# Mixture of softmaxes: two engines copy both column halves to the same partitions, whole-row-pair stores, and six output groups held for the end

## The chip, the cores and the metric

The kernel runs on one core of a Trainium2 chip. The time is device microseconds of one execution. Three runs of the kernel before gave 792.81, 792.83 and 791.32 us, a median of 792.81.

A core has five engines that run side by side and wait for each other by semaphores: TensorE (PE; its weight loads are shown as PEld) multiplies matrices and writes to PSUM, VectorE (DVE), ScalarE (ACT) and GpSimd (POOL) work on tiles, and SyncE (SP) issues transfers. Transfers between DRAM and SBUF are carried by 16 DMA engines. SBUF and PSUM have 128 partitions.

## The reference

For each of 32 x 128 = 4096 rows there are four heads of 4096 logits and four prior weights. A softmax is taken over each head, the prior is turned into a softmax over the heads, and the output row is the weighted sum of the four softmaxes:

```python
prior_probs = np.exp(prior - prior.max(axis=-1, keepdims=True))
prior_probs = prior_probs / prior_probs.sum(axis=-1, keepdims=True)
softmax = np.exp(logits - logits.max(axis=-1, keepdims=True))
softmax = softmax / softmax.sum(axis=-1, keepdims=True)
mixture = np.sum(prior_probs[..., None] * softmax, axis=2)
```

All of it is float32. The logits are 268 MB, the output is 67 MB.

## The kernel before

**Tiles and groups.** The 4096 output rows are cut into 32 groups (g) of 128 rows. A group is two tiles (j = 0, 1) of 64 rows: row m of tile j is row 2m + j of the group, so the two tiles of a group interleave by rows. There are N = 64 tiles; tile n belongs to group n // 2. A tile's load (`load`, L66 to L72, issued by SP at L70) brings 64 rows x 4 heads into 128 partitions: partition 2m + q holds heads 2q and 2q + 1 of row m, 32 KB, 4 MB in all. Five SBUF slots hold tiles. The last six tiles use only slots 4, 0, 1 and 2 (`slot`, L63), so that slot 3 is free from tile 53 on.

**One tile's work.** For each of the two heads i in a partition, `top` (L74) takes the max over 4096 columns on VectorE (L76) and then the exponentials in place on ScalarE, with their sum (L79). `weigh` (L83) takes the reciprocal of the sum on VectorE (L84), makes a 128 x 64 weight matrix on GpSimd from a 0/1 matrix, the reciprocal and the prior's weight (L86), and issues 16 matmuls (L93), 8 pairs of 64 x 512. These add the two partitions of a row and, over i = 0 and 1, the two heads. The column halves of 2048 go to different PSUM partitions: columns 0 to 2047 of the 64 rows stand in partitions 0 to 63 of the accumulator, columns 2048 to 4095 in partitions 64 to 127. There are two accumulators of four PSUM banks, taken in turn.

**Eviction and stores.** `evict` (L112) copies an accumulator to SBUF with one ScalarE instruction of 128 x 2048 (L113). The SBUF buffer `obuf` has 128 partitions x 2 groups' halves; a group's output keeps the column halves on their own partitions. So a store (`store`, L115, through `part`, L100) takes two DMAs of 1 MB, one per column half, each of 64 partitions with two pieces of 8 KB per partition (one for each j). ScalarE issues both.

**The order.** It is written out by hand. The loop of tile n does: `top(n, 0)`; the second half of the tile before, `weigh(w, 1)` with w = n - 1; the load that takes tile w's slot; `top(n, 1)`; `weigh(n, 0)`; then `evict(w)`, and, if w closes a group below `HOLD`, the group's store. Each engine runs its instructions in this order.

**The end.** With `HOLD = G - 4 = 28`, groups 28 and 29 are not stored when they are done: they are kept in slot 3, and their stores are issued after the last load, one column half by SP (in the loop with w = N - 3) and the other by ScalarE (at n = N - 2). Groups 30 and 31 go to `obuf` and are stored in pieces by both queues, the last tile in two halves of 1024 columns.

Of the kernel before, what the change touches and what calls it, by code (L numbers as in the profile page):

```python
# [13 lines left out]
M = 64  # L14
J = 2
Q = 2
BANK = 512
SLOTS = 5


@with_exitstack
def kernel(
    ctx: ExitStack,
    tc: tile.TileContext,
    logits: bass.AP,
    prior: bass.AP,
    out: bass.AP,
):
    nc = tc.nc
    B, S, H, V = logits.shape  # L30
    R = M * J
    G = B * S // R
    N = G * J
    W = V // 2
    assert G * R == B * S and G == 32 and H == 2 * Q and V == 8 * BANK


    lg = logits.rearrange("b s h v -> (b s) h v").rearrange(
        "(g m j) (q i) v -> g j m q (i v)", m=M, j=J, i=Q
    )  # L40
    ov = out.rearrange("b s v -> (b s) v").rearrange("(g m j) v -> g m j v", m=M, j=J)
    pv = prior.rearrange("b s h -> (b s) h").rearrange("(g r) h -> g r h", r=R)

    cpool = ctx.enter_context(tc.tile_pool(name="cpool", bufs=1))
    psum = ctx.enter_context(tc.tile_pool(name="psum", bufs=1, space=bass.MemoryType.PSUM))

    slots = [cpool.tile([P, Q, V], FP32, name=f"slot{i}") for i in range(SLOTS)]

    obuf = cpool.tile([P, J, V], FP32, name="obuf")
    accs = [psum.tile([P, W], FP32, name=f"acc{i}") for i in range(2)]  # L50

    sel = cpool.tile([P, M], FP32, name="sel")
    wts = [[cpool.tile([P, M], FP32, name=f"wt{k}{i}") for i in range(Q)] for k in range(2)]
    pr = cpool.tile([G, R, H], FP32, name="pr")
    pn = cpool.tile([G, J, Q, M, Q], FP32, name="pn")
    pmax = cpool.tile([G, R], FP32, name="pmax")
    pp = cpool.tile([P, J, Q, G], FP32, name="pp")
    nmax = [cpool.tile([P, N], FP32, name=f"nmax{i}") for i in range(Q)]
    dsum = [cpool.tile([P, N], FP32, name=f"dsum{i}") for i in range(Q)]
    rden = [cpool.tile([P, N], FP32, name=f"rden{i}") for i in range(Q)]  # L60


    def slot(n):  # L63
        return slots[n % SLOTS if n < N - 6 else (4, 0, 1, 2)[(n - N + 6) % 4]]

    def load(n):  # L66
        src = lg[n // J, n % J]
        for i in range(0, Q, Q if n < N - 1 else 1):
            k = Q if n < N - 1 else 1
            nc.sync.dma_start(  # L70
                out=slot(n)[:, i : i + k], in_=src[:, :, i * V : (i + k) * V]
            )  # L72

    def top(n, i):  # L74
        x = slot(n)[:, i]
        nc.vector.tensor_reduce(  # L76
            out=nmax[i][:, n : n + 1], in_=x, axis=AX.X, op=ALU.max, negate=True
        )
        nc.scalar.activation(  # L79
            x, x, AF.Exp, bias=nmax[i][:, n : n + 1], accum_out=dsum[i][:, n : n + 1]  # L80
        )

    def weigh(n, i):  # L83
        nc.vector.reciprocal(rden[i][:, n : n + 1], dsum[i][:, n : n + 1])  # L84
        wt = wts[n % 2][i]
        nc.gpsimd.tensor_scalar(  # L86
            out=wt, in0=sel, scalar1=rden[i][:, n : n + 1],
            scalar2=pp[:, n % J, i, n // J : n // J + 1], op0=ALU.mult, op1=ALU.mult,
        )

        for b in range(W // BANK):
            for c in range(2):
                nc.tensor.matmul(  # L93
                    accs[n % 2][c * M : (c + 1) * M, b * BANK : (b + 1) * BANK],
                    lhsT=wt,
                    rhs=slot(n)[:, i, c * W + b * BANK : c * W + (b + 1) * BANK],
                    start=i == 0, stop=i == Q - 1,
                )

    def part(eng, g, c, js=slice(0, J), lo=0, hi=W):  # L100
        eng.dma_start(  # L101
            out=ov[g, :, js, c * W + lo : c * W + hi],
            in_=home(g)[c * M : (c + 1) * M, js, lo:hi],
        )

    HOLD = G - 4

    def home(g):
        x = slots[3] if HOLD <= g < G - 2 else obuf
        return x[:, g % 2].rearrange("p (j w) -> p j w", j=J)  # L110

    def evict(n, lo=0, hi=W):  # L112
        nc.scalar.copy(home(n // J)[:, n % J, lo:hi], accs[n % 2][:, lo:hi])  # L113

    def store(g):  # L115
        for c in range(2):
            part(nc.scalar, g, c)

    def prior_user(n):
        return max(k for k in range(n) if slot(k) is slot(n))  # L120

    with tc.manual_schedule():
        for n in range(SLOTS):
            load(n)
        nc.scalar.dma_start(out=pr, in_=pv)

        nc.gpsimd.memset(sel, 1.0)  # L127
        nc.gpsimd.affine_select(  # L128
            out=sel, in_=sel, compare_op=ALU.is_ge, fill=0.0, base=0,
            pattern=[[-Q, M]], channel_multiplier=1,  # L130
        )
        nc.gpsimd.affine_select(  # L132
            out=sel, in_=sel, compare_op=ALU.is_ge, fill=0.0, base=Q - 1,
            pattern=[[Q, M]], channel_multiplier=-1,
        )

        nc.vector.reduce_max(pmax, pr, axis=AX.X)  # L137
        nc.vector.tensor_sub(pr, pr, pmax.unsqueeze(2).to_broadcast([G, R, H]))  # L138
        nc.scalar.activation(pr, pr, AF.Exp)  # L139
        nc.vector.reduce_sum(pmax, pr, axis=AX.X)  # L140
        nc.vector.reciprocal(pmax, pmax)  # L141
        prv = pr.rearrange("g (m j) (q i) -> g j i m q", j=J, i=Q)
        pmv = pmax.rearrange("g (m j) -> g j m", j=J)
        for j in range(J):
            for i in range(Q):
                nc.vector.tensor_mul(  # L146
                    pn[:, j, i], prv[:, j, i], pmv[:, j].unsqueeze(2).to_broadcast([G, M, Q])
                )
        pq = pn.rearrange("g j i m q -> g j i (m q)")
        for t in range(P // 32):  # L150
            nc.vector.transpose(  # L151
                pp[32 * t : 32 * (t + 1)], pq[:, :, :, 32 * t : 32 * (t + 1)]
            )

        for n in range(N):
            w = n - 1
            top(n, 0)
            if n == N - 2:
                for g in (HOLD, HOLD + 1):
                    part(nc.scalar, g, 1)  # L160
            if w >= 0:
                weigh(w, 1)
                for k in range(SLOTS, N):
                    if prior_user(k) == w:
                        load(k)
                if w == N - 3:
                    for g in (HOLD, HOLD + 1):
                        part(nc.sync, g, 0)
            top(n, 1)
            weigh(n, 0)  # L170
            if w >= 0:
                evict(w)
                g = w // J
                if w % J == J - 1 and g < HOLD:
                    store(g)
                elif w == N - 3 or w == N - 2:
                    js = slice(0, J) if w == N - 3 else slice(0, 1)
                    part(nc.sync, g, 0, js)
                    part(nc.scalar, g, 1, js)

        n = N - 1
        weigh(n, 1)
        for lo in (0, W // 2):
            evict(n, lo, lo + W // 2)
            part(nc.sync, n // J, 0, slice(1, 2), lo, lo + W // 2)
            part(nc.scalar, n // J, 1, slice(1, 2), lo, lo + W // 2)
# [30 lines left out]
```

## Time and profile before

| What | Value |
|---|---|
| Median of three runs | 792.81 us |
| Profiled execution | 793.28 us, span 791.6 us, granted TensorE clock 0.873 |
| Busy, share of the span | PE 69%, DVE 72%, ACT 76%, POOL 7% |
| Bytes | 335.95 MB in all, mean 424 GB/s |
| SP's queue | 272.63 MB, 80.4% of 16 engines' span |
| ACT's queue | 62.98 MB, 19.1% of 16 engines' span |
| VectorE's idle time ahead of the max (L76) | 194.6 us, ended by the loads |
| ScalarE's idle time ahead of the exponentials (L79) | 178.0 us, ended mostly by the max |
| Load of a tile, issue to landing | 38.0 us, median |
| Store of 1 MB by ACT, issue to landing | 21.5 us, median |

The span is the time on the profile's clock between the first and the last event of the program. Engines' busy times overlap, so shares do not add up to one. The line of the DMA engines' use in 40 slices tells whether transfers fill the span; the timeline of one engine tells, in brackets behind an instruction, how long the engine stood idle before it and what ended that.

### The profile page before, as it was taken

The page shows a single profiled execution, that of the slowest core. Times are in us where ns is not written, and L with a number is a line of the kernel's source. Part 1 is how long each engine was busy: PE and PEld are TensorE (multiplying, and loading weights), DVE is VectorE, ACT ScalarE, POOL GpSimd, SP SyncE. Part 2 cuts the span into 40 slices and gives each one's busy share as a digit, 9 for nine tenths or more (in the row PEclk, how much of TensorE's full clock was granted, in tenths as well). Part 3 has the DMA queues.
Part 4 walks back from the last instruction along what each step waited for, and adds up shares of the span by engine and source line. Part 5 has one row for each costly group of instructions (what it writes and reads, how often), then busy time and mean ns, then how long its engine had stood idle before and what let it go on. Part 6 is the DMA issues. An engine that isn't in the chain of part 4 may idle for free.

```text
span 791.6 us, 5426 instructions
## 1 busy us (share of the span) xinstructions
PE 548.0 (69%) x2048; PEld 160.4 (20%) x2048; DVE 573.3 (72%) x268; ACT 600.2 (76%) x323; POOL 51.6 (7%) x135
## 2 busy tenths in 40 slices
PE   0777568776687765767766767677578776687884
PEld 0222112221122221222211222222122221122221
DVE  5986867767768668677686676776867867768890
ACT  1897777787787787877877778778777787787894
POOL 0000000000000000000000000000000000000000
PEclk9999997899978899888999798789997799977897
DMA  9999999999999999999999999999999999999997
GB/s 376 442 416 431 431 428 430 432 431 427 434 432 435 429 432 436 430 433 431 434 429 433 431 431 429 428 435 431 429 431 432 431 432 433 433 430 436 429 416 229
DMA packets 18841, 335.95 MB, mean 424 GB/s; under 512 B 2144, under 2 KB 2144, under 8 KB 2432
## 3 DMA queue, kind: packets, MB, share of 16 engines
q1 hardware_dynamic: 10032, 272.63, 80.4%
q10 hardware_dynamic: 8784, 62.98, 19.1%
q8 instruction: 16, 0.26, 0.1%
q14 instruction: 9, 0.07, 0.0%
HBM read 268.50 MB, written 67.11 MB: 424 GB/s over the span
## 4 chain that ended last, share of the span: by engine, by line
DMA 73%; PE 12%; DVE 10%; ACT 2%; issue 1%; POOL 1%; ACTq 0%; SPq 0%; POOLq 0%
DMA slot<-in_logits_dram 73%; PE acc L93 12%; DVE nmax L76 10%; ACT slot L79 1%; POOL wt L86 1%; ACT obuf L113 1%; ACTq L101 0%; DVE rden L84 0%; SPq L70 0%; POOLq L86 0%; ACTq L79 0%; ACTq L113 0%
## 5 line engine op out<-in xcount | busy, mean ns | idle before, releaser
L93 PE MATMUL acc<-slot,wt 128*64 128x512 f32 x2048 | 548.0, 693 | 235.3 <-POOL wt L86 235.3
L76 DVE TENSOR_REDUCE nmax<-slot 128x1 f32<-128x4096 f32 x128 | 563.5, 4410 | 194.6 <-DMA slot<-in_logits_dram 194.6
L79 ACT ACTIVATE slot<-slot,nmax 128x4096 f32<-128x4096 f32 x128 | 474.6, 3708 | 178.0 <-DVE nmax L76 175.4
L93 PEld LDWEIGHTS acc<-slot,wt 128*64 128x64 f32 x2048 | 160.4, 158 | 622.0 <-POOL wt L86 311.8
L113 ACT COPY obuf<-acc 128x2048 f32<-128x2048 f32 (+1 forms) x61 | 110.9, 1817 | 4.8 <-PE acc L93 4.2
L86 POOL TENSOR_SCALAR wt<-sel,rden,pp 128x64 f32<-128x64 f32 x128 | 50.8, 397 | 725.7 <-DVE rden L84 721.8
L84 DVE RECIPROCAL rden<-dsum 128x1 f32<-128x1 f32 x128 | 19.6, 153 | 6.0 <-ACT slot L79 6.0
L79 ACT ACTIVATION_READ_ACCUMULATOR slot<-slot,nmax 128x1 f32 x128 | 23.9, 186 | 0.0
L113 ACT COPY slot<-acc 128x2048 f32<-128x2048 f32 x4 | 7.4, 1844 | 0.0
L137 DVE TENSOR_REDUCE pmax<-pr 32x128 f32<-32x512 f32 x1 | 0.7, 674 | 2.7 <-DMA pr<-in_prior_dram 2.7
L139 ACT ACT_TABLE_LOAD x1 | 1.3, 1283 | 1.2 <-PEq L201 1.2
L139 ACT ACTIVATE pr<-pr 32x512 f32<-32x512 f32 x1 | 0.6, 628 | 1.6 <-DVE pr L138 1.6
L151 DVE STREAM_TRANSPOSE pp<-pn 32x128 f32<-32x128 f32 x4 | 1.2, 302 | 0.1
L140 DVE TENSOR_REDUCE pmax<-pr 32x128 f32<-32x512 f32 x1 | 0.7, 674 | 0.7 <-ACT pr L139 0.7
L141 DVE RECIPROCAL pmax<-pmax 32x128 f32<-32x128 f32 x1 | 0.9, 942 | 0.0
L146 DVE TENSOR_TENSOR pn<-pr,pmax 32x128 f32<-32x128 f32 x4 | 0.9, 274 | 0.0
L138 DVE TENSOR_TENSOR pr<-pr,pmax 32x512 f32<-32x512 f32 x1 | 0.7, 678 | 0.0
L128 POOL TENSOR_SCALAR_AFFINE_SELECT sel<-sel 128x64 f32<-128x64 f32 x1 | 0.2, 241 | 0.1
L132 POOL TENSOR_SCALAR_AFFINE_SELECT sel<-sel 128x64 f32<-128x64 f32 x1 | 0.2, 240 | 0.1
L127 POOL MEMSET sel<- 128x64 f32 x1 | 0.2, 153 | 0.3 <-POOLq L201 0.3
L201 POOL MEMSET const-float32-0.0<- 128x1 f32 x1 | 0.1, 99 | 0.3 <-issue 0.3
L201 POOL MEMSET const-bfloat16-1.0<- 128x1 bf16 x1 | 0.1, 102 | 0.0
(2 smaller groups left out, 0.2 us busy)
## 6 DMA issues: line engine op xcount, KB each, us to landing
slot<-in_logits_dram SPq DMA_DIRECT2D x63, 4096.0 KB, 38.0
out_dram<-obuf ACTq DMA_DIRECT2D x57, 1024.0 KB, 21.5
slot<-in_logits_dram SPq DMA_DIRECT2D x2, 2048.0 KB, 20.2
out_dram<-slot SPq DMA_DIRECT2D x2, 1024.0 KB, 24.3
out_dram<-slot ACTq DMA_DIRECT2D x2, 1024.0 KB, 12.2
out_dram<-obuf SPq DMA_DIRECT2D x1, 1024.0 KB, 11.2
out_dram<-obuf SPq DMA_DIRECT2D x1, 512.0 KB, 4.3
out_dram<-obuf ACTq DMA_DIRECT2D x1, 512.0 KB, 6.2
```

Source lines behind the costliest of these rows:

```text
L76: nc.vector.tensor_reduce(out=nmax[i][:, n : n + 1], in_=x, axis=AX.X, op=ALU.max, negate=True)
L79: nc.scalar.activation(x, x, AF.Exp, bias=nmax[i][:, n : n + 1], accum_out=dsum[i][:, n : n + 1])
L84: nc.vector.reciprocal(rden[i][:, n : n + 1], dsum[i][:, n : n + 1])
L86: nc.gpsimd.tensor_scalar(out=wt, in0=sel, scalar1=rden[i][:, n : n + 1], scalar2=pp[:, n % J, i, n // J : n // J + 1], op0=ALU.mult, op1= ...
L93: nc.tensor.matmul(accs[n % 2][c * M : (c + 1) * M, b * BANK : (b + 1) * BANK], lhsT=wt, rhs=slot(n)[:, i, c * W + b * BANK : c * W + (b + ...
L113: nc.scalar.copy(home(n // J)[:, n % J, lo:hi], accs[n % 2][:, lo:hi])
L137: nc.vector.reduce_max(pmax, pr, axis=AX.X)
L138: nc.vector.tensor_sub(pr, pr, pmax.unsqueeze(2).to_broadcast([G, R, H]))
L139: nc.scalar.activation(pr, pr, AF.Exp)
L141: nc.vector.reciprocal(pmax, pmax)
L146: nc.vector.tensor_mul(pn[:, j, i], prv[:, j, i], pmv[:, j].unsqueeze(2).to_broadcast([G, M, Q]))
L151: nc.vector.transpose(pp[32 * t : 32 * (t + 1)], pq[:, :, :, 32 * t : 32 * (t + 1)])
```

## The change

Groups 0 to 29 are evicted otherwise. The output buffer gives a group 64 partitions, the even groups the lower and the odd groups the upper ones, and all 2 x 4096 columns of a row pair stand side by side on one partition. So both column halves of an accumulator are copied to the same 64 partitions. The copy is cut at column 1536 (`CUT`, three of the four banks): ScalarE copies 64 x 1536 twice, once per half, and VectorE copies 64 x 512 twice. `declare_no_dep` keeps the two engines from waiting for each other, and dependencies added by hand make each copy wait for the store two groups before, and each store wait for all copies of its group.

A row pair of the output, rows 2m and 2m + 1, is contiguous in DRAM, 32 KB. A group's store is now one DMA of 64 x 32 KB, issued by ScalarE. `HOLD` goes from 28 to 26: groups 26 and 27 stay in `obuf`, 28 and 29 in slot 3, and two DMAs of 4 MB on SP (`store_two`) store them after the last load. Groups 30 and 31 are evicted and stored as before, but into the slot of tile 60 (slot 1), since `obuf` is held.

```diff
+CUT = 3 * BANK
...
-    HOLD = G - 4
+
+    HOLD = G - 6
+    SPLIT = G - 2
+    copies = {}
+    stores = {}
 
     def home(g):
-        x = slots[3] if HOLD <= g < G - 2 else obuf
+        x = obuf if g < G - 4 else slots[3] if g < SPLIT else slot(SPLIT * J)
+        if g < SPLIT:
+            return x[(g % 2) * M : (g % 2 + 1) * M]
         return x[:, g % 2].rearrange("p (j w) -> p j w", j=J)
 
+    def after(ins, other):
+        tc.add_manual_dep(
+            ins.ins, other.ins.name,
+            mybir.DependencyInfo(mybir.DependencyClass.Sync, mybir.DependencyReason.DATA),
+            reason="kept by hand",
+        )
+
+    def apart(ins, g):
+        done = copies.setdefault(g, [])
+        for other in done:
+            if other.ins.engine != ins.ins.engine:
+                tc.declare_no_dep(
+                    ins.ins, other.ins, reason="other columns of the output tile"
+                )
+        if g - 2 in stores:
+            after(ins, stores[g - 2])
+        done.append(ins)
+
     def evict(n, lo=0, hi=W):
-        nc.scalar.copy(home(n // J)[:, n % J, lo:hi], accs[n % 2][:, lo:hi])
+        acc = accs[n % 2]
+        g = n // J
+        dst = home(g)[:, n % J]
+        if g >= SPLIT:
+            nc.scalar.copy(dst[:, lo:hi], acc[:, lo:hi])
+            return
+        for c in range(2):
+            apart(nc.scalar.copy(dst[:, c * W : c * W + CUT], acc[c * M : (c + 1) * M, :CUT]), g)
+        for c in range(2):
+            apart(
+                nc.vector.tensor_copy(
+                    dst[:, c * W + CUT : (c + 1) * W], acc[c * M : (c + 1) * M, CUT:]
+                ),
+                g,
+            )
 
     def store(g):
-        for c in range(2):
-            part(nc.scalar, g, c)
+        stores[g] = nc.scalar.dma_start(out=ov[g], in_=home(g))
+        for ins in copies[g]:
+            after(stores[g], ins)
+
+
+    def store_two(g):
+        x = obuf if g < G - 4 else slots[3]
+        ins = nc.sync.dma_start(
+            out=ov[g : g + 2].rearrange("g m j v -> (g m) j v"), in_=x
+        )
+        for k in (g, g + 1):
+            for other in copies[k]:
+                after(ins, other)
...
             top(n, 0)
-            if n == N - 2:
-                for g in (HOLD, HOLD + 1):
-                    part(nc.scalar, g, 1)
...
                 if w == N - 3:
-                    for g in (HOLD, HOLD + 1):
-                        part(nc.sync, g, 0)
+                    store_two(HOLD)
+                    store_two(HOLD + 2)
```

## The prediction

> **What bounds the kernel now.** I write S(n) for the moment at which VectorE starts the first max of tile n (L76). First the page's slices: are the DMA engines ever idle?
>
> ```profile
> DMA  9999999999999999999999999999999999999997
> GB/s 376 442 416 431 431 428 430 432 431 427 434 432 435 429 432 436 430 433 431 434 429 433 431 431 429 428 435 431 429 431 432 431 432 433 433 430 436 429 416 229
> ```
>
> They are full but for the last slice: transfers bound the body, and the last slice carries 229 GB/s. The stages by window (columns: length, busy time and count of PE, PEld, DVE, ACT, POOL, then clock, DMA share, GB/s):
>
> ```profile
> 23.29:42.71 19.42, 16.54 (x66) 4.79 (x66) 17.75 (x8) 16.80 (x10) 1.59 (x4) 1.00 1.00 432
> 602.00:626.22 24.22, 18.79 (x68) 5.46 (x66) 17.75 (x9) 18.69 (x11) 1.59 (x4) 0.79 1.00 430
> 735.27:754.70 19.43, 15.75 (x66) 4.65 (x64) 17.75 (x9) 16.47 (x11) 1.58 (x4) 0.91 0.99 428
> 776.00:791.60 15.60, 7.23 (x28) 2.02 (x24) 0.16 (x1) 5.07 (x5) 0.40 (x1) 0.72 0.68 194
> ```
>
> A pair of tiles with its output group (602 row) takes 24.22 us, 12.1 us a tile; where no stores run (23 and 735 rows) a tile takes 9.71 us. In the last 15.6 us the DMA share is 0.68: here the last tile's arithmetic is awaited. So the end is a race between transfers and the compute chain. That chain by VectorE's timeline:
>
> ```profile
> 735.27 4.42 DVE L76 TENSOR_REDUCE nmax<-slot 128x1 f32<-128x4096 f32 x1 [2.90 <-DMA slot<-in_logits_dram]
> 739.61 0.15 DVE L84 RECIPROCAL rden<-dsum 128x1 f32<-128x1 f32 x1
> 739.68 4.40 DVE L76 TENSOR_REDUCE nmax<-slot 128x1 f32<-128x4096 f32 x1
> 743.99 0.15 DVE L84 RECIPROCAL rden<-dsum 128x1 f32<-128x1 f32 x1
> 745.00 4.42 DVE L76 TENSOR_REDUCE nmax<-slot 128x1 f32<-128x4096 f32 x1 [0.85 <-DMA slot<-in_logits_dram]
> 754.70 4.42 DVE L76 TENSOR_REDUCE nmax<-slot 128x1 f32<-128x4096 f32 x1 [0.83 <-DMA slot<-in_logits_dram]
> ```
>
> VectorE needs 8.8 us of a tile and then waits for the load. TensorE's timeline (one line per unbroken burst; 32 are the last half of tile n-1 and the first of tile n):
>
> ```profile
> 619.25 9.85 PE L93 MATMUL acc<-slot,wt 128*64 128x512 f32 x32 [3.33 <-POOL wt L86]
> 643.47 3.65 PE L93 MATMUL acc<-slot,wt 128*64 128x512 f32 x16 [3.33 <-POOL wt L86]
> 740.40 8.78 PE L93 MATMUL acc<-slot,wt 128*64 128x512 f32 x32 [2.00 <-POOL wt L86]
> 759.84 3.65 PE L93 MATMUL acc<-slot,wt 128*64 128x512 f32 x16 [1.67 <-POOL wt L86]
> ```
>
> Sixteen matmuls take 3.65 us at full clock (F); in a merged burst the first sixteen take 8.78 - 3.65 = 5.13 (M) or about 9.85 - 3.65 = 6.2 (S, clock low from the start). From 520 to 630 us nine successive tiles are two F, five M, two S. ScalarE's PSUM copies by shape:
>
> ```profile
> L113 ACT COPY obuf<-acc 128x2048 f32<-128x2048 f32 x59 | 108.8, 1845 | 0.0
> L113 ACT COPY obuf<-acc 128x1024 f32<-128x1024 f32 x2 | 2.0, 1012 | 4.8 <-PE acc L93 4.2 <-ACT obuf L113 0.6
> ```
>
> **The change part by part.** *The split eviction on ScalarE.* 60 copies of 2048 columns become 120 of 1536: by the two rows 1012 + 512 x 0.813 ns = 1.43 us each, 2.86 a tile for 1.85, +1.0 us x 60. ScalarE's tile is then 2 x 3.71 + 2.86 = 10.3 us (plus 0.6 us of DMA issue in every second), under the 12.1 us of the body: hidden there by its idle time before L79 (178 us), and in the last stage by VectorE's chain below. Were that cover gone, it would pace the last stage at 10.3 us.
>
> *The new work on VectorE.* 120 copies of 512 columns. No row shows VectorE reading PSUM. The page's nearest in engine and columns:
>
> ```profile
> L138 DVE TENSOR_TENSOR pr<-pr,pmax 32x512 f32<-32x512 f32 x1 | 0.7, 678 | 0.0
> ```
>
> I take 2 x 0.678 = 1.35 us a tile. Ends: below, 512 columns at the max's rate (4.34/4096) without fixed cost, 2 x 0.54 = 1.1; above, each with another 0.18 us, the fixed part of ScalarE's PSUM copy (2 x 1.012 - 1.845), 2 x 0.86 = 1.72.
>
> *The new wait.* These copies wait for the last sixteen matmuls of tile n-1, and behind them on VectorE stands the max of tile n+1, for which ScalarE's exp waits. The matmuls start 740.40 - 735.27 = 5.13 us after S(n) and end at 8.78 (F), 10.26 (M) or 11.3 (S); the reciprocal ahead of the copies ends at 743.99 + 0.15 - 735.27 = 8.87. So VectorE needs per tile C = 10.2 (F: 8.87 + 1.35), 11.6 (M) or 12.7 (S). In the body the mix gives (2 x 10.2 + 5 x 11.6 + 2 x 12.7)/9 = 11.5 us against 12.1: the loads still set the pace, with 0.6 us to spare, and a late tile costs nothing since loads land 38 us after issue, three tiles ahead. ScalarE's new wait for VectorE's copies before a store is over before its own end (S(n) + 15.5).
>
> *The stores.* One 2 MB issue in place of two of 1 MB: ScalarE's queue loses one issue of 0.6 us per group, which its idle time hid. 32 KB against 32 KB packets of loads should give a store half the engines where 8 KB against 32 KB gave it a fifth: a store is through in about 10 us, not 24. The bytes per second: a pair with stores moves 10.49 MB in 24.22 us = 433 GB/s, loads alone 4.194/9.71 = 432, so 8 KB packets cost nothing now and I take 0. Ends: the ACT queue's bytes at the SP queue's price (19.1% for 62.98 MB against 80.4% for 272.63) would save 2.8% of 151 us, of it 26/32 groups, -3.4 us; the lowest slice of the body (427 for 431) laid to the stores alone, a fifth of the bytes, +1.4.
>
> *Two more groups held.* Before the last loads 2 x 2.097 MB less is moved: 4.194/0.431 = 9.7 us. Tile 62 would land at 745.0 for 754.7, and tiles 55 on every 9.7 us, as long as their slots are free: load 63 goes out after the last matmul of tile 59, S(60) + 10.3 = 742.5 at the C taken below, still before 745.0. But VectorE now paces these tiles. S(54): 662.57 now; the store of group 25, issued at 652.75 and at a fifth, was 40% through then; at half it is through, 0.6 x 2.097/0.431 = 2.9 us more ahead of tile 54: S(54) = 665. Copies run in loops 54 to 60, seven of them: S(61) = 665 + 7C against 745.0. After tile 61 VectorE has no more copies and ScalarE is the chain as before, with the loads already there: the 0.39 us before the exp at 763.54 and some 0.1 go, -0.5. End moved by 7C - 80.5.
>
> Which C? After idle times of TensorE of up to 1.67 us every burst was F, after 1.95 to 2.26 us M, S only after 3.3 or more. The idle time here is C less the burst, 2.2 (F) to 2.9 us (M): no S, and mostly M. I take the body's ratio, five M to two F: C = 11.2, S(61) = 743.4, **-2.1 us**. All M: C = 11.6, +0.7. All F: 10.2, -9.1, cut by the drain.
>
> [...] The burst at 740.40, after 2.00 us, ran slow at first, so I go by the row.
>
> *The drain.* Loads end at 745.0 + 9.7 = 754.7; the six groups, 12.58 MB/0.431 = 29.2 us, end at 783.9, and at least 3.0 us (shortest landing of a store) follow: 786.9 for 791.6, so no gain over 4.7 us. The first 4 MB store stands on SP right behind the last load, the second waits for tile 59's copies (S(59) + 15.5 = 736.5), early enough; behind them are only the last groups' halves. The last pieces, issued about then, share the engines with little.
>
> **Sum.** The profiled run took 793.28 (span 791.6 and 1.7 around it), 0.5 above the median 792.81. 793.28 - 2.1 - 0.5 = 790.7.
>
> **Rivals.** [...] *A wash*: C between 11.3 and 11.7, all or nearly all M; -1.6 to +1.6, 791.2 to 794.4; for it the M after every idle time of two us. *VectorE becomes the bound* (other side): the pair of copies costs p. From p = 1.47 with all M (10.26 + p), or 1.87 with five M, C is 11.73 and the end later by 0.2%: +1.6 us, 794.4. At the upper end p = 1.72, all M: C = 12.0, +3.4 us, 796.2. From p = 1.95 (C = 12.1 in the body) the body itself falls behind: each 0.1 us costs 5.8 us more, and a longer tile lengthens TensorE's idle time towards S, 1.1 us a tile; p = 2.05, all M, gives 7 x 12.3 - 80.5 + 5.8 = +11.4, 804.2. For it: no row shows this copy, and the margin is 0.6 us; against it: the 512-column rows. *Better packets*: -3.4 more, 787.3; against it the equal rates.
>
> **How the numbers follow.** Forecast as told (a gain of 1.6 to 4.7 us with C from 10.8 to 11.27): 0.34; drain or better packets: 0.12; wash: 0.18; VectorE the bound: 0.36. So faster by over 0.2% 0.46, within (1.6 us, about what a measurement of this kernel tells from no change) 0.18, slower 0.36. The forecast's own range is 788.1 to 791.2. With both signs held, the range goes from 787.3 (better packets) to 799, between the last two prices of the VectorE case; beyond lie some 0.2.
>
> **What would show it.** VectorE copies near 0.68 us x120 and ScalarE's near 1.43 x120; tiles still 12.1 us apart in the body, with loads ending VectorE's waits; from tile 54 on VectorE idle for TensorE and not for loads, S(61) near 743; a DMA share near 1 until about 784. Wrong if a VectorE copy takes 0.8 us or more, if S is common after 660 us, or if the body's pair takes other than 24.2 us.

## The result, and the profile after

The changed kernel takes 829.22 us (four runs, 828.75 to 834.09), the kernel before 792.07 us (791.11 to 792.83 beside them): a ratio of 1.048, 95% interval 1.044 to 1.053. It is 37 us slower, where 2 us less was forecast. The profiled run took 834.09 us (span 832.4), 41 us over that of before. A run more than 1.5% above the fastest of its kernel is left out of medians and ratios; of the runs told here this concerns one of e5.

First the slices of the page, as before: are the DMA engines idle, and what do they move?

```profile
DMA  9999999999999999999999999999999999698997
GB/s 381 430 424 416 413 431 419 412 417 409 430 398 418 414 403 414 412 409 406 411 402 421 406 415 418 406 413 409 397 418 427 415 419 392 287 392 355 412 402 269
```

They are as full as before in the body, but the row of rates has changed from 430 or so in every slice to values between 397 and 431. A late VectorE would leave gaps; busy engines that move less point elsewhere. Now two windows of the changed kernel with the columns of the prediction (length, busy time and count of PE, PEld, DVE, ACT, POOL, then clock, DMA share, GB/s). The first lies ahead of the first store, which is issued at 50.1 us; the second reaches from the start of tile 8 to that of tile 52:

```profile
23.29:42.71 19.42, 16.45 (x56) 4.79 (x58) 18.33 (x9) 17.03 (x10) 1.19 (x3) 0.91 1.00 432
107.93:681.11 573.18, 381.95 (x1418) 111.31 (x1414) 450.88 (x265) 463.65 (x268) 34.90 (x88) 0.85 1.00 413
```

And the same 44 tiles in the kernel before:

```profile
102.90:638.33 535.43, 381.53 (x1410) 111.69 (x1408) 390.55 (x176) 411.55 (x221) 34.89 (x88) 0.86 1.01 432
```

Loads alone still run at 432 GB/s. As soon as stores run, the rate is 413 for 432, at a DMA share of 1.00 (1.01 before): 573.2 us for 535.4, 38 us more, or 0.86 us a tile. Tile 8 itself starts 5 us later (107.93 for 102.90). From tile 52 to the end the changed kernel needs 151.3 us against 153.3. The three parts, 5.0 + 37.8 - 2.0, are the 40.8 us between the spans. (The other three runs of the changed kernel took 828.75 to 829.58 us; so some 5 us of the 41 are this run's own.) The loss lies in the stretches where stores of 2 MB run beside loads, and the rest, from tile 52 on, got 2 us shorter.

The groups of the page say what VectorE waited for (columns: busy time, mean ns of one, then idle time ahead of them and what ended it):

```profile
L77 DVE TENSOR_REDUCE nmax<-slot 128x1 f32<-128x4096 f32 x128 | 563.3, 4408 | 64.0 <-DMA slot<-in_logits_dram 63.3
L145 ACT COPY obuf<-acc 64x1536 f32<-64x1536 f32 x112 | 160.5, 1433 | 2.0
L148 DVE COPY obuf<-acc 64x512 f32<-64x512 f32 x112 | 77.2, 689 | 83.7 <-PE acc L94 81.3
```

Both copies have the predicted price: 1433 ns for 1.43 us, 689 ns for 0.678. VectorE now waits 81.3 us for TensorE ahead of its copies, the wait of which the prediction spoke, and still 63.3 us for loads ahead of the max. An engine that waits for loads is not the bound, though it lost most of its 194.6 us of such waits.

### The profile page after: what moved, and what is told of

It is laid out like the page before. It is cut to its first block, busy times and chain, and to the rows that moved or that the text cites. A ratio compares the mean times of both kernels' runs of the same rounds, so it can differ in the third digit from the quotient of the medians.

```text
span 832.4 us, 5668 instructions
## 1 busy us (share of the span) xinstructions
PE 548.6 (66%) x2048; PEld 160.0 (19%) x2048; DVE 655.4 (79%) x388; ACT 666.8 (80%) x383; POOL 51.6 (6%) x135
## 4 chain that ended last, share of the span: by engine, by line
DMA 61%; DVE 16%; PE 15%; ACT 4%; issue 2%; POOL 1%; ACTq 0%; POOLq 0%; SPq 0%
DMA slot<-in_logits_dram 61%; PE acc L94 15%; DVE nmax L77 14%; ACT slot L80 3%; DVE obuf L148 1%; POOL wt L87 1%; ACT obuf L145 1%; ACT slot L142 1%; DVE slot L148 1%; ACT slot L145 0%; DVE rden L85 0%; ACTq L102 0%; POOLq L87 0%; SPq L71 0%; ACTq L80 0%
## 5 line engine op out<-in xcount | busy, mean ns | idle before, releaser
L77 DVE TENSOR_REDUCE nmax<-slot 128x1 f32<-128x4096 f32 x128 | 563.3, 4408 | 64.0 <-DMA slot<-in_logits_dram 63.3
L145 ACT COPY obuf<-acc 64x1536 f32<-64x1536 f32 x112 | 160.5, 1433 | 2.0
L148 DVE COPY obuf<-acc 64x512 f32<-64x512 f32 x112 | 77.2, 689 | 83.7 <-PE acc L94 81.3
L145 ACT COPY slot<-acc 64x1536 f32<-64x1536 f32 x8 | 11.5, 1434 | 0.1
L142 ACT COPY slot<-acc 128x2048 f32<-128x2048 f32 (+1 forms) x5 | 7.6, 1517 | 4.8 <-PE acc L94 4.2
L148 DVE COPY slot<-acc 64x512 f32<-64x512 f32 x8 | 5.5, 689 | 3.1 <-PE acc L94 3.0
## 6 DMA issues: line engine op xcount, KB each, us to landing
out_dram<-obuf ACTq DMA_DIRECT2D x26, 2048.0 KB, 16.8
```

The costliest lines, as they stand in the source:

```text
L77: nc.vector.tensor_reduce(out=nmax[i][:, n : n + 1], in_=x, axis=AX.X, op=ALU.max, negate=True)
L142: nc.scalar.copy(dst[:, lo:hi], acc[:, lo:hi])
L145: apart(nc.scalar.copy(dst[:, c * W : c * W + CUT], acc[c * M : (c + 1) * M, :CUT]), g)
L148: nc.vector.tensor_copy(dst[:, c * W + CUT : (c + 1) * W], acc[c * M : (c + 1) * M, CUT:]),
```

## The experiments

The question after the result: do the stores themselves slow the transfers, or does the longer chain of VectorE, ScalarE and TensorE hold the loads back? And if it is the stores, which of their properties does it: the length of a packet, the number of partitions, their place, or the rows in DRAM?

### Part by part in the whole kernel

**e1_8k_stores: the packets of before under the new copies.**

```diff
-        stores[g] = nc.scalar.dma_start(out=ov[g], in_=home(g))
+        stores[g] = [nc.scalar.dma_start(
+            out=ov[g, :, :, c * W : (c + 1) * W], in_=home(g)[:, :, c * W : (c + 1) * W])
+            for c in range(2)]
...
```

> The changed kernel with only the body's stores cut: each group is stored by two 1 MB transfers of 64 partitions x 2 pieces of 8 KB, one per column half, as in the kernel before; copies on both engines, layout and the six held groups stay. Transfer theory (the long store packets slow the DMA engines: 411 GB/s in the changed kernel's body for 431): a pair of tiles is back at 24.2 to 24.5 us and the time at 790 to 797 us. VectorE theory (its chain of max, wait for TensorE and copies paces the body): nothing of that chain is changed, so 824 to 832 us.

Measured: 796.41 us (791.64 to 797.56), 1.0037 [1.0018, 1.0057]. All but 3 to 4 of the 37 us are gone, with every copy of the changed kernel still there. What is left has a likely cause in the trace. In the view of the output buffer's instructions, these are the waits of their engines (us and times), the first by what ended it, the second by who waited:

```profile
  DMA out_dram<-obuf: 37.4, 20
...
  DVE obuf L148: 37.4, 20
```

A store cut into 8 KB pieces takes 25.0 us to land (16.8 in the changed kernel), and VectorE's copies two groups later waited for one 20 times. That these waits make up what is left was not tested.

**e2_16k_stores: one DMA per row of the pair, 64 x 16 KB each.**

```diff
-        stores[g] = nc.scalar.dma_start(out=ov[g], in_=home(g))
+        stores[g] = [nc.scalar.dma_start(out=ov[g, :, j], in_=home(g)[:, j]) for j in range(J)]
...
```

> The changed kernel with each group's store cut into two transfers of 64 x 16 KB, one per row of the pair. Transfer theory with a loss that grows with the packet: between the 8 KB version and the changed kernel, 800 to 820 us; if any packet over 8 KB does it, 825 to 832. VectorE theory: 824 to 832 us.

Measured: 791.64 us (789.69 to 794.47), 0.9996 [0.9982, 1.0010], no difference to the kernel before, and less than either theory had expected. The window from tile 8 to 52 again, of this run:

```profile
104.50:640.13 535.63, 376.80 (x1410) 109.62 (x1408) 450.89 (x266) 460.32 (x265) 34.59 (x88) 0.87 1.00 432
```

and the max's row among its groups:

```profile
L77 DVE TENSOR_REDUCE nmax<-slot 128x1 f32<-128x4096 f32 x128 | 563.2, 4407 | 35.4 <-DMA slot<-in_logits_dram 34.7
```

432 GB/s, and 12.17 us a tile as before. VectorE has the same busy time as in the changed kernel (450.9) and keeps 35.4 us of waiting for loads over 64 tiles, 0.55 us a tile: the margin of 0.6 us that the prediction gave it. So VectorE does stay inside the tile. The whole change with stores of 16 KB packets is a wash.

**e5_act_copies: all copies on ScalarE, none on VectorE, 32 KB stores kept.**

```diff
-            apart(nc.scalar.copy(dst[:, c * W : c * W + CUT], acc[c * M : (c + 1) * M, :CUT]), g)
-        for c in range(2):
-            apart(
-                nc.vector.tensor_copy(
...
+            apart(nc.scalar.copy(dst[:, c * W : (c + 1) * W], acc[c * M : (c + 1) * M]), g)
```

> The changed kernel with VectorE's copies given to ScalarE: two copies of 64 x 2048 per tile, 1.85 us each by the row of the 128x2048 copy; 32 KB stores and six held groups stay. VectorE theory: VectorE's chain is as before the change, ScalarE needs 7.4 + 3.7 = 11.1 us a tile, so the body returns to 24.2 us a pair: 790 to 800 us. Transfer theory: the stores are the same, so the body stays at about 25.5 us a pair, 822 to 834 us.

Measured: 829.78 us (three runs, 827.79 to 838.11; a fourth took 843.21), 1.0499 [1.0435, 1.0562], as slow as the changed kernel. VectorE's copies are not what costs the time.

**f1_32k_in_two: the same 32 KB packets in two DMAs of 32 partitions each.**

```diff
-        stores[g] = nc.scalar.dma_start(out=ov[g], in_=home(g))
+        stores[g] = [nc.scalar.dma_start(
+            out=ov[g, r * 32 : (r + 1) * 32], in_=home(g)[r * 32 : (r + 1) * 32])
+            for r in range(2)]
...
```

> The changed kernel with each group's store cut into two transfers of 32 partitions x 32 KB: same packets, two transfers as in the 16 KB version. P (packet size): as the changed kernel, 822 to 834 us. Rival D (one transfer per group, not its packet size, is what costs): as the 16 KB version, 789 to 795 us.

Measured: 812.15 us (810.19 to 817.59), 1.0278 [1.0240, 1.0316]: about half of the loss, between the two ranges that were expected. Packet length and total bytes are those of the changed kernel, so the shape of the DMA matters as well.

### The transfers alone

To take the engines out altogether, the next kernels keep only the loads in their order and the stores, held in place by one-column copies. Each of the later ones differs from the first, t32_transfers, in a line or two.

**t32_transfers, t16_transfers, t128_transfers.** The store of a group is, in turn, that of the changed kernel (64 partitions, the lower and the upper half in turn), that of e2, and one of 128 partitions for two groups together. The store in t32_transfers:

```python
nc.scalar.dma_start(out=ov[g], in_=home2(g))
```

What takes its place in t16_transfers and, second, in t128_transfers:

```diff
+                for j in range(J):
+                    nc.scalar.dma_start(out=ov[g, :, j], in_=home2(g)[:, j])
...
+                if g % 2 == 1:
+                    nc.scalar.dma_start(
+                        out=ov[g - 1 : g + 1].rearrange("g m j v -> (g m) j v"), in_=obuf)
```

> Transfers alone: the loads of all 64 tiles into the five slots, and per group one store of 64 partitions x 32 KB, sent by ScalarE once the group's second load has landed (a one-column copy makes the order). All arithmetic and the prior's load are left out, so the output is not computed. Theory P (the 32 KB store packets beside the loads slow the DMA engines by themselves): the changed kernel's body rate of 411 GB/s, 335.9 MB in about 817 us and 4 to 8 us of ends, 818 to 828 us. Rival C (they are slow only beside the compute engines' traffic in SBUF): 432 GB/s, 780 to 788 us.

> The same transfers alone with each group stored by two transfers of 64 x 16 KB. P and C both: 432 GB/s, 780 to 788 us.

> The same transfers alone with two groups stored by one transfer of 128 partitions x 32 KB. P (packet size): as slow as with 64 partitions, 815 to 830 us. Rival H (the burst reads one half of the partitions only): 432 GB/s, 780 to 790 us.

Measured: 826.28, 786.05 and 783.51 us (ratios to before 1.0433 [1.0410, 1.0457], 0.9925 [0.9905, 0.9945], 0.9893 [0.9873, 0.9913]). Without any arithmetic the loss is all there: 42.8 us between t32 and t128, 1.34 us for each of 32 stores. The changed kernel has 26 such stores, and 26 x 1.34 = 35 us is its 37 us within the two. And packets of 32 KB are not slow as such: t128 has them and is 43 us faster. Of the 2.5 us between t16 and t128 little is lost in the body: between 100 and 700 us they move 432 and 433 GB/s.

**ts_even_partitions, td_dram_stride, tl16_short_loads.** Three single changes of t32: the store reads every second partition (and the one-column copy writes there); the store keeps its partitions but its rows lie 64 KB apart in DRAM; the stores stay and the loads are cut into 16 KB packets. In this order:

```diff
-                nc.scalar.dma_start(out=ov[g], in_=home2(g))
+                nc.scalar.dma_start(out=ov[g], in_=obuf[g % 2 :: 2])
...
-                nc.scalar.dma_start(out=ov[g], in_=home2(g))
+                nc.scalar.dma_start(
+                    out=ov[g - g % 2 : g - g % 2 + 2].rearrange("t m j v -> (t m) j v").rearrange(
+                        "(m t) j v -> t m j v", t=2)[g % 2],
+                    in_=home2(g))
...
-        for i in range(0, Q, Q if n < N - 1 else 1):
-            k = Q if n < N - 1 else 1
+        for i in range(Q):
+            k = 1
```

> Transfers alone as in the run with one 64 x 32 KB store per group (826 us), but the 64 source partitions are every second one of the 128, even for even groups and odd for odd ones; the DRAM side is unchanged. All arithmetic is left out. Theory S (SBUF side: long packets from one half of the partitions crowd the same part of SBUF): 432 GB/s again, 781 to 790 us. Rival R (DRAM side: where 16 engines write at once): unchanged, 815 to 830 us.

> Transfers alone as in the run with one 64 x 32 KB store per group, source partitions in one half as there, but neighbouring partitions write row pairs 64 KB apart in DRAM, so that two groups interleave there. All arithmetic is left out. Theory S (SBUF side): unchanged, 815 to 830 us. Rival R (DRAM side): 781 to 790 us.

> Transfers alone with one 64 x 32 KB store per group, and the loads in two transfers of 128 x 16 KB per tile. All arithmetic is left out. If the long store packets are slow whatever stands beside them: 815 to 832 us. If it takes long packets on both sides: 780 to 790 us.

Measured: 783.31, 827.26 and 881.11 us (0.9892 [0.9874, 0.9910], 1.0447 [1.0427, 1.0467], 1.1127 [1.1068, 1.1186]). So it is the SBUF side: the same number of packets of the same length from spread partitions costs nothing, and moving the rows in DRAM changes nothing. Shorter load packets make it worse, beyond both ranges that were expected: 389 GB/s between 100 and 700 us. They are not slow by themselves. Before the first store of this run, issued at 18.41 us, has packets under way, the loads alone move (length, then clock, DMA share, GB/s at the end):

```profile
10.00:20.00 10.00, 0.00 (x0) 0.19 (x1) 0.00 (x0) 1.00 1.01 434
```

**tm_middle_partitions, tl_lower_half.** What was left open is which property of the 64 partitions decides, and there were two theories: that they are neighbours, or that they lie on one side of partition 64.

```diff
-                nc.scalar.copy(obuf[h, 0, 0:1], slot(w)[h, 0, 0:1])
-                nc.scalar.dma_start(out=ov[g], in_=home2(g))
+                nc.scalar.copy(sel[:, 0:1], slot(w)[:, 0, 0:1])
+                nc.scalar.dma_start(out=ov[g], in_=obuf[32:96])
```

tl_lower_half has `obuf[0:64]` in the last line.

> Only the transfers again, with no arithmetic but one-column copies, and the output is left at zero. The store of every group is one DMA of 64 x 32 KB, out of partitions 32 to 95 for all groups: as many neighbouring partitions as in the slow kernels (826 us with partitions 0 to 63 and 64 to 127 in turn), but half of them below and half of them above partition 64. [...] Theory N (neighbouring partitions of any place slow the stream): 826 us (820 to 832), 412 GB/s. [...]

> The control of the run beside it: the same transfers-only kernel, with the store of every group out of partitions 0 to 63 (64 x 32 KB, output left at zero), never out of the upper half, and with no copy that waits for an earlier store. Both theories: slow as the kernel that takes the halves in turn, 826 us (818 to 835), about 412 GB/s between 100 and 700 us. If it is fast (783 us), the turn of the halves or the waits for earlier stores are what the other kernels were slowed by, and both theories fall.

Measured: 783.38 us (783.10 to 783.66; 0.9886 [0.9871, 0.9900]) out of partitions 32 to 95, and 821.27 us (820.62 to 824.61; 1.0373 [1.0343, 1.0402]) out of 0 to 63. Sixty-four neighbours cost nothing when half of them lie on either side of partition 64. One side alone is slow, whether it is always the lower (38 us more) or each in turn (43 us). Between 100 and 700 us the first moves 433 GB/s, the second 414. The page's rows of the queues, where q1 carries SP's loads and q10 ScalarE's stores (packets, MB, share of 16 engines' span), out of partitions 32 to 95, span 781.3 us:

```profile
q1 hardware_dynamic: 9360, 268.44, 79.9%
q10 hardware_dynamic: 2560, 67.11, 19.9%
```

The two halves in turn (t32_transfers), 412 GB/s in the same window, span 825.5 us:

```profile
q1 hardware_dynamic: 9360, 268.44, 78.1%
q10 hardware_dynamic: 2560, 67.11, 21.3%
```

Packets and bytes are the same. The stores' packets take 0.213 x 825.5 - 0.199 x 781.3 = 20.4 us more of all engines' time, and the loads' packets 0.781 x 825.5 - 0.799 x 781.3 = 20.5 us more. So the loads, which have nothing to do with the stores' buffer, are stretched as much in sum as the stores. The traces' records of single packets, between 100 and 700 us, show that most packets are not stretched at all: the median 32 KB packet takes 1.21 us in both runs. But 11% of the loads' and 17% of the stores' in t32_transfers take over 1.05 times that, up to 2.7 and 4.0 us; out of partitions 32 to 95, and in t16_transfers, almost none do. In the changed kernel it is 11% of the loads' and 20% of the stores' 32 KB packets, up to 3.0 and 3.6 us, with the same median of 1.21 us; in the kernel before, where the stores' packets have 8 KB, 0.1% of the loads' and 0.4% of the stores' take over 1.05 times their medians of 1.21 and 0.31 us. The queues of the whole kernels show the same, first the changed one (span 832.4 us), then e2 (span 792.3 us):

```profile
q1 hardware_dynamic: 10032, 278.93, 80.9%
q10 hardware_dynamic: 2512, 56.69, 17.2%
```

```profile
q1 hardware_dynamic: 10032, 278.93, 82.4%
q10 hardware_dynamic: 4592, 56.69, 16.9%
```

For the same bytes SP's queue (the loads and the held stores) takes 0.809 x 832.4 - 0.824 x 792.3 = 20.6 us more of all engines' time, and ScalarE's 0.172 x 832.4 - 0.169 x 792.3 = 9.3 us more.

**Why the length counts.** Here the runs end and an argument begins. They show where the dividing line lies: 0 to 63 slow (821.27 us), 32 to 95 and every second one fast (783.38 and 783.31 us). They also show the order of the losses by the packets: none to be seen at 8 KB out of one side (e1, 432 GB/s between 100 and 640 us), 2.5 us over t128 at 16 KB, 42.8 us at 32 KB, and 97.6 us at 32 KB beside loads of 16 KB, which t128 does not have. The stores' median times from issue to landing go with it only in part. Each of a group's two transfers of 1 MB took 25.0 us in 8 KB packets (e1) and 16.5 us in 16 KB packets (e2), so longer packets got a store through sooner; but 2 MB in 32 KB packets out of one side took 16.8 us in the changed kernel, no less. With the transfers alone it was 16.3 us out of one side (t32_transfers) and 14.2 us out of every second partition (ts_even_partitions), some 129 and 148 GB/s, as an estimate from these times and 2.1 MB. The author's argument is that stores of longer packets ask for more than one side of partition 64 delivers beside the loads, and that both queues then wait. No run shows how much one side can deliver, nor how the engines share their time between the packets of two queues, nor why 32 KB out of one side costs 43 us where 16 KB is nearly free (786.05 us); that stays argued.

### The end of the kernel

**e3_hold6_alone: the kernel before, with six groups held and nothing else.** Groups 26 and 27 stay in `obuf`, 28 and 29 in slot 3, 30 and 31 in the slot of tile 60.

```diff
-    HOLD = G - 4
+    HOLD = G - 6
-        x = slots[3] if HOLD <= g < G - 2 else obuf
+        x = obuf if g < G - 4 else slots[3] if g < G - 2 else slot(N - 4)
...
-                    for g in (HOLD, HOLD + 1):
+                    for g in range(HOLD, HOLD + 4):
```

> The kernel before with only the hold changed: groups 26 and 27 stay in the output buffer, 28 and 29 in slot 3, 30 and 31 go to tile 60's slot; one ScalarE copy per tile and 8 KB store pieces as before. Both theories: the body keeps 24.2 us a pair. The last loads land 9.7 us earlier; ScalarE and VectorE need 9.2 to 9.8 us a tile there, so the end comes forward by up to the drain's bound of 4.7 us: 787.5 to 790.5 us. If the hold itself costs something, 792 or more.

Measured: 789.59 us (789.29 to 789.77), 0.9965 [0.9952, 0.9978]. It beats both kernels, the one before by 2.7 us. Its slices:

```profile
DMA  9999999999999999999999999999999999999998
GB/s 376 433 430 433 433 428 431 433 432 429 428 431 430 432 430 435 433 434 431 428 433 430 430 430 431 433 427 431 431 433 437 427 433 434 433 437 426 426 415 311
```

The last slice carries 311 GB/s where it carried 229: the stores that were held fill the time in which the last tile is worked on.

**g1_copies_later: e2 with VectorE's copies of a tile put one tile later.** `evict_v` holds the two VectorE copies, taken out of `evict`; the store follows them. The wait of VectorE for TensorE then falls away.

```diff
+            if w >= 1 and (w - 1) // J < SPLIT:
+                evict_v(w - 1)
+                g = (w - 1) // J
+                if w % J == 0 and g < HOLD:
+                    store(g)
...
```

> The 16 KB version (791.6 us) with VectorE's copies of tile n - 1 put behind the max of tile n + 1 instead of ahead of it, and the group's store behind them; bytes, packets and copies unchanged. Theory W (with the transfers repaired, the last stage is paced by VectorE's wait for TensorE that stands ahead of the max): the wait goes, VectorE needs 10.2 us a tile and ScalarE 10.3 there, the first max of tile 61 comes 5 to 8 us earlier and the end reaches the drain's bound, 788 to 790 us. Rival X (the copies' time alone sets that stage, or it is the drain already): 791 to 793 us.

Measured: 791.62 us (790.22 to 794.13), 0.9999 [0.9988, 1.0010]. VectorE's timeline in the last stage, first of e2:

```profile
738.93 4.40 DVE L77 TENSOR_REDUCE nmax<-slot 128x1 f32<-128x4096 f32 x1
743.25 0.15 DVE L85 RECIPROCAL rden<-dsum 128x1 f32<-128x1 f32 x1
744.76 1.39 DVE L148 COPY slot<-acc 64x512 f32<-64x512 f32 x2 [1.35 <-PE acc L94]
746.18 4.42 DVE L77 TENSOR_REDUCE nmax<-slot 128x1 f32<-128x4096 f32 x1
```

and of g1_copies_later:

```profile
740.05 4.40 DVE L77 TENSOR_REDUCE nmax<-slot 128x1 f32<-128x4096 f32 x1
744.48 1.39 DVE L153 COPY slot<-acc 64x512 f32<-64x512 f32 x2
745.90 0.16 DVE L85 RECIPROCAL rden<-dsum 128x1 f32<-128x1 f32 x1
745.98 4.40 DVE L77 TENSOR_REDUCE nmax<-slot 128x1 f32<-128x4096 f32 x1
```

The 1.35 us of waiting for TensorE are gone. A tile of this stage takes 10.3 to 10.6 us (tiles 56 to 61), where e2's took 11.7 on the mean (54 to 61), and the first max of tile 61 starts at 740.05 us instead of 746.18, the 5 to 8 us earlier that theory W expected. But the time is what rival X expected: the medians of e2 and g1 agree within 0.1 us, with a scatter of 4 to 5 us in each. The mechanism is shown in the trace, its worth in the time is not, and where the gain goes was not found.

## Why the prediction was wrong

**The step that failed** is the one on the stores: "8 KB packets cost nothing now and I take 0", with ends of -3.4 and +1.4 us for the longer packets. Measured, the 32 KB stores out of one side cost some 38 us (after against e2, whose stores have 16 KB packets: 829.22 - 791.64 = 37.6), some twenty-seven times the upper end. Both ends were taken from rows in which stores of 8 KB are mixed with loads, that is from the old packet length. The trace held no store from one side of SBUF with packets as long as the loads', and the bounds did not reach past that. The upper end also charged the lowest slice to the stores' fifth of the bytes alone, while the runs show the loads losing as much as the stores (20.5 and 20.4 us). The remark that a store "should" get half the engines was used for its landing alone, and no run shows the half. Before, ScalarE's queue took a fifth (20.4% of 16 engines' time from 602.00 to 626.22 us); after, a store landed in 16.8 us, where about 10 was foretold, and even out of every second partition in 14.2 (ts_even_partitions). It was not asked whether 64 partitions on one side can deliver half of 432 GB/s beside the loads; in t32_transfers they delivered some 129, by the estimate above.

**The body.** "The loads still set the pace" held: VectorE waits 63.3 us for loads. That "the body's pair takes other than 24.2 us" would refute the forecast was the right test: it takes 2 x 13.03 = 26.1 us. In e2 it is 2 x 12.17 = 24.3.

**The copies.** ScalarE's 1.43 us a copy and VectorE's 1.35 us a tile were right (1.433; 1.39 to 1.41 for a pair in the timeline). ScalarE's tile of 10.3 us left out the reading of each sum, which makes an exponential 3.80 us from start to end instead of 3.71, and the tile 10.5; it stayed under cover. So the rival that had the other side, VectorE the bound with p above 1.47, did not come about: the sign that it foresaw came from another mechanism, and e5, without VectorE's copies, is as slow.

**The last stage.** VectorE's timeline of the changed kernel has the wait where it was foretold, on its copies, and none for loads:

```profile
750.23 1.39 DVE L148 COPY slot<-acc 64x512 f32<-64x512 f32 x2 [1.59 <-PE acc L94]
751.54 4.40 DVE L77 TENSOR_REDUCE nmax<-slot 128x1 f32<-128x4096 f32 x1
761.80 1.39 DVE L148 COPY slot<-acc 64x512 f32<-64x512 f32 x2 [1.40 <-PE acc L94]
772.00 1.39 DVE L148 COPY slot<-acc 64x512 f32<-64x512 f32 x2
```

From tile 54 (707.00 us) to tile 61 (784.18 us) a tile takes 11.0 us on the mean, for C = 11.2, and from tile 52 to the end the kernel gains 2.0 us, for 2.1. That is this run's. In e2, where the loss of the stores is gone, C is 11.7, as in the all-M case; the prediction's own sum, 7 x 11.7 - 80.5, makes that 1.4 us later, and e2's profiled run is 1.1 us longer than that of before (794.36 for 793.28). Over all runs e2 gains 0.3 us [-0.8, +1.4], by the interval of its ratio: the wash, which had 0.18. So with a right price for the stores the forecast would have been 1 us off (790.7 for e2's 791.64), but partly by luck, since its C was not the one of that run.

**Holding six groups.** The drain's bound of -4.7 was not reached; alone it gives -2.7 us (e3). With the split copies and 16 KB stores beside it, in e2, that gain is gone. The traces have it lost in the last stage, where tile 61 starts at 735.05 us in e3 and at 746.18 in e2, and the stretch from tile 52 to the end takes 149.8 and 152.2 us. That the copies alone do it is likely, but g1 did not show it in the time.

**The bursts after idle times.** Going by the row, the burst at 740.40 that ran slow at first after 2.00 us, was right. TensorE's timeline after (32 are two times sixteen matmuls without a break):

```profile
723.79 3.65 PE L94 MATMUL acc<-slot,wt 128*64 128x512 f32 x16 [3.07 <-POOL wt L87]
734.14 3.65 PE L94 MATMUL acc<-slot,wt 128*64 128x512 f32 x16 [2.30 <-POOL wt L87]
744.84 8.78 PE L94 MATMUL acc<-slot,wt 128*64 128x512 f32 x32 [2.31 <-POOL wt L87]
756.67 8.52 PE L94 MATMUL acc<-slot,wt 128*64 128x512 f32 x32 [3.05 <-POOL wt L87]
768.24 3.65 PE L94 MATMUL acc<-slot,wt 128*64 128x512 f32 x16 [3.06 <-POOL wt L87]
```

After 2.31 us of idle time the first sixteen took 8.78 - 3.65 = 5.13 us, slow as in that row. But the reading behind the wash, a slow burst after every idle time of two us, falls too: after 2.30, 3.06 and 3.07 us three were at full speed, 3.65 us for sixteen (as one had been after 3.33 us in the prediction's own rows). The length of the gap alone does not decide, and what does was not found. The mix that was taken was near the truth in this run (11.0 for 11.2) and half a us short in e2.

## What to carry to other kernels

Before the packets of a store are made longer, ask how such a store runs beside the other queue, and whether its partitions lie on both sides of partition 64: 64 x 32 KB out of one side cost 1.34 us per 2 MB store here (1.2 where it was always the lower side), out of partitions 32 to 95, of every second one or of all 128 nothing. The low rate at a DMA share of 1.00 (413 GB/s for 432) pointed to the transfers themselves, and a kernel with the transfers alone settled it in one run (826.28 us). Where a trace shows no row for a new shape of DMA, the bounds must go well past the rows that it has.

## What was not expected of the hardware

- Stores of 32 KB packets out of one side of partition 64 slowed loads that fill all 128 partitions, by as much time in sum as they were slowed themselves (20.5 and 20.4 us, t32_transfers against tm_middle_partitions), while the engines showed as busy (412 GB/s at a DMA share of 1.00). Only a minority of the packets was stretched, 11% and 17% there, 11% and 20% in the changed kernel.
- The loss depended on both packet lengths: with 32 KB loads, stores of 16 KB cost 2.5 us (t16 over t128), of 32 KB 42.8 us (t32); with 16 KB loads, which alone run at 434 GB/s, the run with 32 KB stores is 97.6 us over t128 (tl16_short_loads).
- The same packets as two DMAs of 32 partitions lost only about half as much (812.15 us for 829.22, 792.07 before). Why, no run shows.
